# Gate projections of a merged three-branch block as seven half-sized products a gate

## The chip, the cores and the metric

The kernel runs on one core of one Trainium2 chip. A core has five engines with a queue of instructions each: TensorE (PE, matrix products), VectorE (DVE), ScalarE (ACT), GpSimd (POOL) and SyncE (SP, which issues most transfers). The metric is the device time of one execution in microseconds (us), as the median of several runs.

## What is computed

One layer of a decoder trunk on 512 tokens of 1024 features, in float32. Three token mixers give three branches of 512 features; each is mapped to 1024 features, weighted by a sigmoid gate computed from the normalised input, and the three are added. The change lies in the lines from `gates` to `merged`.

```python
h = rms_norm(x, g_mix)                       # 512 tokens x 1024
p = h @ w_in                                 # 1024 x 7680
q, fp, iv, go, bg, cg, xc, u, v, gates = jnp.split(p, offsets, axis=-1)
...
z = jnp.stack([o_a, o_b, o_c], axis=2)       # three branches of 512 features
y = jnp.einsum('bsnw,nwd->bsnd', z, w_branch)          # 3 x (512 -> 1024)
gate = jax.nn.sigmoid(gates).reshape(B, S, N_BRANCH, D)
merged = jnp.sum(gate * y, axis=2)
x = x + merged @ w_o
h2 = rms_norm(x, g_ffn)
x = x + jnp.square(jax.nn.relu(h2 @ w_ff1)) @ w_ff2
return rms_norm(x, g_final)
```

## The kernel before

Every float32 operand is split into a high part (rounded to the type fp32r, on ScalarE) and a low part (the rest, on VectorE), and a product of two operands takes three matmuls, high by high, high by low and low by high (`mm3`). A matmul has 128 partitions and 512 columns.

The work is a list of *units*. A unit is what one weight tile of 128 x 1024 is used for: 24 matmuls (8 pairs of blocks by 3). The main loop goes through the list. At unit i it lets ScalarE make the high part of the weights of unit i + 2, takes the result of unit i - 1 out of PSUM (its *take-in*), lets VectorE make the low part, issues the next loads on SP, and then issues the matmuls of unit i. Two tables of hooks add other work by hand: `pre` ahead of a unit's matmuls and `post` behind them. Each engine works through its queue in the order in which the loop writes it. Raw weight tiles (tag `raw`), high parts (`wh`) and low parts (`wl`) have three buffers each, PSUM accumulators (`acc`) eight; other tiles have one buffer with a name of its own (`x0`.., `z0`.., `h0`..), and who takes such a buffer again waits for its last reader.

In order, the units are: projections of the first mixers; 12 units of the short convolution; then, eight times (d is a block of 128 output features), three gate projections of one unit each, the products of branches 1 and 2 in one unit (`w_bc`) and that of branch 0 in half a unit (`w_a`); eight units of the output projection `w_o`; and the feed-forward stage. Gates and merged values are *feature-major*: features on the partitions, tokens along the columns. The merged block d is split into `mg`, and the output projection takes it as the stationary operand.

The normalised input is not stored. `xh` and `xl` hold x times `g_mix`, split; a gate's result is multiplied by `rb`, the reciprocal root mean square of each token along the columns, when it is taken in (`ev_gate`):

```python
tt(dve, g, a, rb, ALU.mult)
act.activation(g, g, AF.Sigmoid)
```

The feed-forward stage already uses seven products of half-sized blocks in place of eight, with weight sums formed by transfers that add to what is in a tile (issued by POOL, `accum_op`). Its output stage turns tiles from token-major to feature-major by transposes on PE, 16 in a group (`turn`), in two groups.

Of the kernel before, what the change touches and what calls it, by code (L numbers as in the profile page):

```python
# [11 lines left out]
ALU = mybir.AluOpType  # L12
# [21 lines left out]


@with_exitstack
def trunk_kernel(ctx: ExitStack, tc, xT, x_t, w_f, w_t, w_bc, w_a, w_o, w_1, w_2, vecs, rows, gfin, w_sg, cst, lmask, out):
# [522 lines left out]
    for d in range(KD):  # L560
        for n in (1, 2, 0):
            proj(28 + n * KD + d, lambda a, d=d, n=n: ev_gate(d, n, a))
        unit(w_bc[d], lambda w: (branch(w, 0, 1), branch(w, S, 2)), lambda a, d=d: ev_bc(d, a))
        unit(w_a[d], lambda w: branch(w, 0, 0), lambda a, d=d: ev_a(d, a), S)
# [603 lines left out]
```

## Time and profile before

| | before |
|---|---|
| device time, median of 3 runs | 829.73 us (828.86 to 830.4) |
| profiled execution: its device time, and its span | 829.05 us, 827.3 us |
| PE busy, matmuls | 816.8 us, 99% |
| PE busy, loading weights (PEld, beside the matmuls) | 682.6 us, 83% |
| VectorE busy | 543.8 us, 66% |
| ScalarE busy | 346.0 us, 42% |
| GpSimd busy | 156.2 us, 19% |
| bytes moved by transfers | 102.45 MB |

The profile is one execution, and its own device time lies 1.75 us above its span. A busy share is a mean over the span. Matmuls are pipelined, so that the printed length of one is longer than the distance from its start to the next one's.

### The profile page before, as it was taken

What the parts mean: (1) busy time and instruction counts of PE and PEld (TensorE: products, weight loads), DVE (VectorE), ACT (ScalarE), POOL (GpSimd) and SP (SyncE); (2) the same over time, 40 slices, a digit from 0 to 9 for tenths busy, and PEclk for the clock granted to TensorE, in tenths of its full rate; (3) what the DMA queues carried; (4) which work ended last, traced back from release to release, by engine and by line L of the source; (5) the groups of instructions that cost most, each with busy time, mean ns of one, the idle gap of its engine ahead of it and who ended that gap; (6) DMA issues with size and microseconds to landing.
All of it is one profiled execution on the core that took longest, in us unless ns stands there. A gap on an engine that the chain in (4) does not pass through costs nothing.

```text
span 827.3 us, 9867 instructions
## 1 busy us (share of the span) xinstructions
PE 816.8 (99%) x3798; PEld 682.6 (83%) x3798; DVE 543.8 (66%) x706; ACT 346.0 (42%) x519; POOL 156.2 (19%) x187
## 2 busy tenths in 40 slices
PE   9999999999999999999999999999999999999995
PEld 7888888888988888888888888888888888888884
DVE  7556999878664445544454445777777777777763
ACT  6567555354333223223232335343434343434332
POOL 4313555561220000000000010302020202020000
PEclk9999999999999999999999999999999999999998
DMA  8331232213113232232325345748393839383502
GB/s 312 124 103 52 76 107 72 77 52 102 58 58 103 94 110 90 90 96 95 115 89 204 103 156 149 216 116 238 93 247 88 248 87 246 89 239 96 162 1 101
DMA packets 30432, 102.45 MB, mean 124 GB/s; under 512 B 3505, under 2 KB 3889, under 8 KB 30385
## 3 DMA queue, kind: packets, MB, share of 16 engines
q1 hardware_dynamic: 20736, 67.45, 23.7%
q0 software_dynamic: 9360, 34.08, 16.8%
q8 instruction: 30, 0.49, 0.3%
q10 hardware_dynamic: 288, 0.29, 0.1%
q14 instruction: 18, 0.14, 0.1%
HBM read 99.71 MB, written 2.10 MB: 123 GB/s over the span
## 4 chain that ended last, share of the span: by engine, by line
PE 91%; DVE 4%; ACT 3%; issue 1%; POOLq 0%; POOL 0%; DVEq 0%; ACTq 0%
PE acc L98 28%; PE acc L100 28%; PE acc L99 28%; PE acc L1058 3%; PE acc L326 3%; DVE h L79 1%; DVE wl L79 1%; DVE h L307 1%; ACT h L257 1%; DVE h L270 0%; ACT wh L972 0%; PE acc L989 0%; ACT h L261 0%; PE acc L478 0%; PE acc L379 0%
## 5 line engine op out<-in xcount | busy, mean ns | idle before, releaser
L98 PE MATMUL acc<-x,wh 128*128 128x512 f32 x672 | 263.8, 393 | 0.3 <-DVE h L332 0.3
L100 PE MATMUL acc<-x,wl 128*128 128x512 f32 x672 | 261.6, 389 | 0.0
L99 PE MATMUL acc<-x,wh 128*128 128x512 f32 x672 | 261.5, 389 | 0.0
L972 ACT ACTIVATE wh<-raw 128x1024 fp32r<-128x1024 f32 (+1 forms) x114 | 116.7, 1026 | 239.6 <-PE acc L99 136.3
L79 DVE TENSOR_TENSOR wl<-raw,wh 128x1024 fp32r<-128x1024 f32 (+1 forms) x120 | 152.1, 1269 | 44.3 <-ACT wh L972 43.9
L100 PEld LDWEIGHTS acc<-x,wl 128*128 128x128 f32 x672 | 126.1, 188 | 26.5
L98 PEld LDWEIGHTS acc<-x,wh 128*128 128x128 f32 x672 | 126.2, 188 | 26.1 <-DVE h L332 0.5
L99 PEld LDWEIGHTS acc<-x,wh 128*128 128x128 f32 x672 | 126.2, 188 | 25.8 <-issue 0.2
L79 DVE TENSOR_TENSOR h<-h,acc 128x512 f32<-128x512 f32 x118 | 75.7, 682 | 11.1 <-PE acc L100 10.9
L79 DVE TENSOR_TENSOR z<-z,z 128x1024 fp32r<-128x1024 f32 x51 | 61.7, 1221 | 32.1 <-ACT z L766 32.1
L692 ACT ACTIVATE h<-tmp 128x512 f32<-128x512 f32 x32 | 20.3, 634 | 124.9 <-DVE tmp L691 124.9
L766 ACT ACTIVATE z<-z 128x1024 fp32r<-128x1024 f32 x51 | 53.1, 1052 | 45.7 <-PE acc L100 28.2
L79 DVE TENSOR_TENSOR h<-h,h 128x256 f32<-128x256 f32 (+4 forms) x89 | 66.8, 755 | 7.6 <-ACT h L745 3.6
L100 PE MATMUL acc<-z,h 128*128 128x512 f32 x184 | 71.6, 389 | 0.0
L99 PE MATMUL acc<-z,h 128*128 128x512 f32 x184 | 71.6, 389 | 0.0
L98 PE MATMUL acc<-z,h 128*128 128x512 f32 x184 | 71.6, 389 | 0.0
L79 DVE TENSOR_TENSOR tmp<-acc,rb 128x512 f32<-128x512 f32 x28 | 19.4, 691 | 79.0 <-PE acc L100 79.0
L762 POOL DMA_DIRECT2D z<-w x28 | 24.6, 877 | 232.5 <-DVE z L79 192.9
L79 POOL TENSOR_TENSOR tmp<-tmp,tmp 128x512 f32<-128x512 f32 x15 | 21.1, 1405 | 198.0 <-DVE tmp L79 185.9
L691 DVE SCALAR_TENSOR_TENSOR tmp<-acc,rb 128x512 f32<-128x512 f32 x32 | 22.0, 688 | 30.8 <-PE acc L100 30.8
L100 PEld LDWEIGHTS acc<-z,h 128*128 128x128 f32 x184 | 34.5, 188 | 7.3
L99 PEld LDWEIGHTS acc<-z,h 128*128 128x128 f32 x184 | 34.5, 188 | 7.2
(187 smaller groups left out, 1070.3 us busy)
## 6 DMA issues: line engine op xcount, KB each, us to landing
z<-w POOLq DMA_DIRECT2D x65, 512.0 KB, 6.5
raw<-w_f SPq DMA_DIRECT2D x52, 512.0 KB, 3.3
raw<-w SPq DMA_DIRECT2D x34, 512.0 KB, 5.3
raw<-w_bc SPq DMA_DIRECT2D x8, 512.0 KB, 3.3
raw<-w_o SPq DMA_DIRECT2D x8, 512.0 KB, 3.3
raw<-w_t SPq DMA_DIRECT2D x4, 512.0 KB, 3.2
raw<-w_a SPq DMA_DIRECT2D x8, 256.0 KB, 2.6
h<-x_t SPq DMA_DIRECT2D x4, 512.0 KB, 7.1
```

Of the source, the lines that this page charges most:

```text
L79: return e.tensor_tensor(out=o, in0=a, in1=b, op=op)
L98: pe.matmul(o, lh, rh, start=start, stop=False, skip_group_check=more)
L99: pe.matmul(o, lh, rl, start=False, stop=False, skip_group_check=more)
L100: pe.matmul(o, ll, rh, start=False, stop=stop, skip_group_check=more)
L257: act.activation(d["t1"], d["t1"], AF.Exp, scale=-1.0)
L326: pe.matmul(ps[:, cs(b)], kl[:, cs(b)], qk[:, cs(b)], start=True, stop=True)
L691: dve.scalar_tensor_tensor(out=t, in0=part["f", i], scalar=0.0, in1=part["r2b"], op0=ALU.max, op1=ALU.mult)
L692: act.activation(hf["a" if r < 2 else "b"][:, cs(r % 2, S)], t, AF.Square)
L762: pool.dma_start(wr[n, g], w_2[g, src[0], src[1]], accum_op=ALU.add)
L766: act.activation(hi, wr[src, g], AF.Copy)
L972: act.activation(hi[:, :n], raws[i][:, :n], AF.Copy)
L1058: pe.matmul(a4[t], lh, rh, start=j == 0 and rnd == 0, stop=j == KD - 1 and rnd == 2)
```

## The change

Each gate is now token-major (tokens on the partitions) and made by seven products. The normalised input X (512 x 1024) is cut into four blocks X11, X12, X21, X22 of 256 tokens x 512 features, and a gate's weights W into W11 to W22 of 512 features x 512 outputs. Four combinations of X blocks ("1" = X21 - X22, "2" = "1" - X11, "4" = "2" + X12, "3" = X11 - X21) and four sums of W blocks (t1 = W12 + W11, t2 = t1 + W22, t4 = t2 + W21, t3 = W12 + W22) are formed, and the products are, in the order of `G_ORDER`, p1 = X11 W11, p5 = "1" t1, p2 = X12 W21, p6 = "2" t2, p3 = "4" W22, p7 = "3" t3, p4 = X22 t4. Some are added to an accumulator that is left open in PSUM. Each has 24 matmuls.

For this x is loaded a second time, unsplit, 512 features at a time (*half* g = 0, 1; each holds half of every block's features) into the tiles h0 and h1 (`x_load`), normalised there (`x_norm`), and its seven combinations are formed and split into tiles h2 to h15 (`x_form`). SP loads the weight blocks (`g_load`) and a first block of a sum (`g_chain`, tags x0 to x7, which were the slots of `xh` and `xl` and are now in pairs), GpSimd adds blocks to it (`g_add`), and ScalarE and VectorE split each (`g_split`).

The order of the units behind the convolutions is now: four units of branch 1 (y1), the seven products of gate 1, those of gate 2, four units of branch 2 (y2), gate 0's seven, and five of branch 0 (y0, the last one halved). Branch products are token-major as well; `y_ev` and `merge_1` multiply and add. The merged tiles are transposed on PE (`m_turn`, two groups of 16) and split (`m_turned`) for the output projection. Loads of units are held back between y1 and gate 0 (`limit`). The host arranges the weights to match (`w_g`, `w_b`).

```diff
-    def ev_gate(d, n, a):
-        g = tmp()
-        part[n] = g
-        tt(dve, g, a, rb, ALU.mult)
-        act.activation(g, g, AF.Sigmoid)
...
-    def ev_bc(d, a):
-        for i, n in enumerate((1, 2)):
-            tt(dve, part[n], a[i], part[n], ALU.mult)
-        tt(pool, part[1], part[1], part[2], ALU.add)
-
-    def ev_a(d, a):
-        tt(dve, part[0], a, part[0], ALU.mult)
-        tt(dve, part[0], part[0], part[1], ALU.add)
-        mt = hslot(d, F32R)
-        act.activation(mt[:, :S], part[0], AF.Copy)
-        yield
-        tt(dve, mt[:, S:], part[0], f(mt[:, :S]), ALU.subtract)
-        mg.append((mt[:, :S], mt[:, S:]))
+    def x_load(g):
+        for i in range(2):
+            xr_[i] = hslot(i, F32)
+            for b in range(2):
+                nc.sync.dma_start(xr_[i][:, cs(b, S)], xT[4 * g + 2 * i + b])
+
+    def x_norm(g):
+        for b in range(4):
+            xv = xr_[b // 2][:, cs(b % 2, S)]
+            dve.scalar_tensor_tensor(out=xv, in0=xv, scalar=vcol(V_GMIX + 4 * g + b), in1=rb, op0=ALU.mult, op1=ALU.mult)
+
+    def x_form(g, *names):
+        def q(i, half):
+            return two(xr_[i])[:, :, half * 256:(half + 1) * 256]
+        for n in names:
+            if n in ("11", "12", "22"):
+                src = q(int(n[1]) - 1, int(n[0]) - 1)
+            else:
...
+                tt(dve, src, i0, i1, op)
+                xr_[n] = src
+            t = hslot(XT[g, n], F32R)
+            hi, lo = two(t[:, :S]), two(t[:, S:])
+            act.activation(hi, src, AF.Copy)
+            tt(dve, lo, src, f(hi), ALU.subtract)
+            xf[g, n] = (hi, lo)
...
+    def g_chain(n, kind, base):
+        for g in range(2):
+            gw[n, g, kind] = xpair(base + g, F32)
+            nc.sync.dma_start(gw[n, g, kind], w_g[n, g, 0, 1])
+
+    def g_add(n, kind, fi, c):
+        for g in range(2):
+            pool.dma_start(gw[n, g, kind], w_g[n, g, fi, c], accum_op=ALU.add)
...
+    def g_product(n, a, b, key, start):
+        if start:
+            part[key] = [acc() for _ in range(2)]
+        for j in range(2):
+            for g in range(2):
+                for p in range(2):
+                    ah, al = (x[:, p, cs(j)] for x in xf[g, a])
+                    bh, bl = (x[:, cs(p, S)] for x in gw[n, g, b, "r"])
+                    mm3(part[key][j], ah, al, bh, bl, start and g == 0 and p == 0, g == 1 and p == 1, not start)
+
+    G_ORDER = (("p1", "11", "11", "B", True), ("p5", "1", "t1", "C", True), ("p2", "12", "21", "A", True),
+               ("p6", "2", "t2", "B", False), ("p3", "4", "22", "C", False), ("p7", "3", "t3", "B", False),
+               ("p4", "22", "t4", "B", False))
...
+    def g_ev(p):
...
+            if p in ("p1", "p5"):
+                act.activation(v, a, AF.Copy)
+            elif p == "p6":
+                act.activation(v, a, AF.Copy, scale=-1.0)
+            elif p == "p4":
+                act.activation(v, a, AF.Sigmoid)
+            else:
+                tt(dve, v, v, a, ALU.subtract if p == "p7" else ALU.add)
+                act.activation(v, v, AF.Sigmoid)
...
+    def y_ev(n, c):
+        for t in range(4):
...
+            if n == 1:
+                act.activation(v, part["y"][t], AF.Copy)
+            else:
+                tt(dve, v, v, part["y"][t], ALU.mult)
+                tt(dve, m, m, v, ALU.add)
+
+    def merge_1():
+        for t in range(4):
+            tt(dve, mt[t], mt[t], gt[t], ALU.mult)
+
+    def m_turn(ks):
+        for k in ks:
+            part["m", k] = acc()
+            for t in range(4):
+                pe.transpose(part["m", k][:, cs(t)], mt[t][:, cs(k)], ident)
...
+    at(pre, y1 - 2, x_load, 0)
+    at(pre, y1 - 1, x_norm, 0)
+    at(pre, y1 - 1, x_form, 0, "11")
+    at(pre, y1, x_form, 0, "1", "2", "12")
+    at(pre, y1 + 1, x_form, 0, "4", "3", "22")
+    at(pre, y1 + 1, x_load, 1)
+    at(pre, y1 + 2, x_norm, 1)
+    at(pre, y1 + 2, x_form, 1, "11")
+    at(pre, y1 + 3, x_form, 1, "1")
+    at(pre, y1 + 4, x_form, 1, "2", "12")
+    at(pre, y1 + 5, x_form, 1, "4")
+    at(pre, y1 + 6, x_form, 1, "3", "22")
...
+    def g_sched(n, c, t3, first):
+        u = gu[n]
+        at(pre, u - 1, g_split, n, "11", W11)
+        at(pre, u, g_split, n, "t1", ("c",))
+        at(pre, u, g_add, n, "c", *W22)
+        at(pre, u + 1, g_split, n, "21", W21)
+        at(pre, u + 2, g_split, n, "t2", ("c",))
+        at(pre, u + 2, g_add, n, "c", *W21)
+        if first:
+            at(pre, u + 2, g_chain, n, "t3", t3)
+            at(pre, u + 2, g_add, n, "t3", *W22)
+        at(pre, u + 3, g_split, n, "22", W22)
+        at(pre, u + 4, g_split, n, "t3", ("t3",))
+        at(pre, u + 5, g_split, n, "t4", ("c",))
...
+    at(pre, u2, merge_1)
...
+    at(post, y0 + 3, m_turn, range(4))
+    at(pre, y0 + 4, m_turned, range(4))
+    at(post, o0, m_turn, range(4, KD))
+    at(pre, o0 + 1, m_turned, range(4, KD))
```

What that makes of the queues is shown at three places, as engine rows with the names that the program gives its tiles (a number behind a name only tells tiles of one name apart). First VectorE's queue behind the last convolution unit, before: `tmp<-acc,tmp` is the result of the convolution, `z` its low part, `wl` the low part of a unit's weights, and `tmp<-acc,rb` a gate that is taken in.

```order
L79 TENSOR_TENSOR tmp_2083<-acc_2099,tmp_2083 128x512
L79 TENSOR_TENSOR wl_2125<-raw_2040,wh_2124 128x1024
L79 TENSOR_TENSOR z_2128<-tmp_2083,z_2128 128x512
L79 TENSOR_TENSOR tmp_2162<-acc_2134,rb 128x512
L79 TENSOR_TENSOR wl_2160<-raw_2097,wh_2159 128x1024
L79 TENSOR_TENSOR tmp_2196<-acc_2168,rb 128x512
L79 TENSOR_TENSOR wl_2194<-raw_2132,wh_2193 128x512
```

The same place of the change, from the last low part of the heads (`z`) on. The tiles h_2032 and h_2035 are h0 and h1 with half 0 of x, normalised by the two rows of L540; h_2099 is "11", then come "1", "2" and "12".

```order
L85 TENSOR_TENSOR z_2092<-h_507,z_2092 128x512
L540 SCALAR_TENSOR_TENSOR h_2032<-h_2032,vec,rb 128x512 x2
L540 SCALAR_TENSOR_TENSOR h_2035<-h_2035,vec,rb 128x512 x2
L85 TENSOR_TENSOR h_2099<-h_2032,h_2099 128x512
L85 TENSOR_TENSOR tmp_2081<-acc_2104,tmp_2081 128x512
L85 TENSOR_TENSOR wl_2130<-raw_2038,wh_2129 128x1024
L85 TENSOR_TENSOR z_2133<-tmp_2081,z_2133 128x512
L85 TENSOR_TENSOR tmp_2137<-h_2032,h_2035 128x512
L85 TENSOR_TENSOR h_2139<-tmp_2137,h_2139 128x512
L85 TENSOR_TENSOR tmp_2142<-tmp_2137,h_2032 128x512
L85 TENSOR_TENSOR h_2144<-tmp_2142,h_2144 128x512
L85 TENSOR_TENSOR h_2147<-h_2035,h_2147 128x512
```

It goes on with a branch's weights, then "4", "3" and "22" of half 0, and half 1 of x (h_2199 and h_2202, again h0 and h1), its "11" and "1", and the split of W11, whose two tiles are raw_2207 and raw_2209.

```order
L85 TENSOR_TENSOR wl_2183<-raw_2102,wh_2182 128x1024
L85 TENSOR_TENSOR tmp_2186<-tmp_2142,h_2035 128x512
L85 TENSOR_TENSOR h_2188<-tmp_2186,h_2188 128x512
L85 TENSOR_TENSOR tmp_2191<-h_2032 128x512
L85 TENSOR_TENSOR h_2193<-tmp_2191,h_2193 128x512
L85 TENSOR_TENSOR h_2196<-h_2035,h_2196 128x512
L540 SCALAR_TENSOR_TENSOR h_2199<-h_2199,vec,rb 128x512 x2
L540 SCALAR_TENSOR_TENSOR h_2202<-h_2202,vec,rb 128x512 x2
L85 TENSOR_TENSOR h_2249<-h_2199,h_2249 128x512
L85 TENSOR_TENSOR tmp_2280<-h_2199,h_2202 128x512
L85 TENSOR_TENSOR h_2282<-tmp_2280,h_2282 128x512
L85 TENSOR_TENSOR wl_2286<-raw_2207,wh_2285 128x1024
```

Where VectorE had one take-in and one low part in each unit, the normalising, summing and splitting of x has moved in between, ahead of the low part of W11. Second, SP's queue at the same place, with what each transfer waits for in brackets (an engine, or a queue of transfers). Before, it holds a unit's weights each time:

```order
L964 DMA raw_2040<-w_f 128x1024 [waits DMAHW5_49,DVE_49]
L964 DMA raw_2097<-w_bc 128x1024 [waits DMAHW6_49,DVE_49]
L964 DMA raw_2132<-w_a 128x512 [waits DMAHW7_49,DVE_49,Activation_49]
L964 DMA raw_2166<-w_f 128x1024 [waits DMAHW0_49,DVE_49]
```

After, between the loads of branch 1 and those of W11 (raw_2207, raw_2209), it holds the first blocks of the chain (x_2150, x_2152) and half 1 of x:

```order
L1189 DMA raw_2102<-w_b 128x1024 [waits DMAHW6_49]
L572 DMA x_2150<-w_g 128x1024 [waits PE_49]
L572 DMA x_2152<-w_g 128x1024 [waits DMAHW7_49,PE_49]
L535 DMA h_2199<-xT 128x512 [waits DMAHW0_49,DVE_49,Activation_49]
L535 DMA h_2199<-xT 128x512 [waits DMAHW1_49]
L535 DMA h_2202<-xT 128x512 [waits DMAHW2_49,DVE_49]
L535 DMA h_2202<-xT 128x512 [waits DMAHW3_49]
L567 DMA raw_2207<-w_g 128x1024 [waits DMAHW4_49]
L567 DMA raw_2209<-w_g 128x1024 [waits DMAHW5_49]
```

The loads of half 1 wait for VectorE and ScalarE (the last readers of h0 and h1), and those of W11 stand behind them. Third, VectorE at the second product of gate 0 after the change: `z` are the gate tiles of branch 2, `x` the merged tiles, and the last two rows the low parts of gate 0's t1.

```order
L85 TENSOR_TENSOR z_2674<-z_2674,acc_2992 128x512
L85 TENSOR_TENSOR x_2237<-x_2237,z_2674 128x512
L85 TENSOR_TENSOR z_2675<-z_2675,acc_2993 128x512
L85 TENSOR_TENSOR x_2239<-x_2239,z_2675 128x512
L85 TENSOR_TENSOR z_2676<-z_2676,acc_2994 128x512
L85 TENSOR_TENSOR x_2241<-x_2241,z_2676 128x512
L85 TENSOR_TENSOR z_2677<-z_2677,acc_2995 128x512
L85 TENSOR_TENSOR x_2243<-x_2243,z_2677 128x512
L85 TENSOR_TENSOR wl_3065<-x_2848,wh_3064 128x1024
L85 TENSOR_TENSOR h_3069<-x_2850,h_3068 128x1024
```

At a gate unit before, VectorE had one take-in and one low part (the rows of L79 above); here eight operations of 512 columns stand ahead of the low part.

## Rows read from the trace of the kernel before

**Rows 1.** The page, part 1: busy time, share of the span, instructions.

```profile
PE 816.8 (99%) x3798; PEld 682.6 (83%) x3798; DVE 543.8 (66%) x706; ACT 346.0 (42%) x519; POOL 156.2 (19%) x187
```

**Rows 2.** Waits of TensorE: total us, times, longest us.

```profile
PE acc L989 <- DVE ones L982: 1.1, 1, 1.1
PE acc L98 <- DVE h L332: 0.3, 1, 0.3
```

**Rows 3.** Timeline of PE (start us, us, line): first projection and first transposes.

```profile
245.04 0.39 PE L98 MATMUL acc<-x,wh 128*128 128x512 f32 x1
...
468.08 0.38 PE L641 MATMUL acc<-cons,h 128*128 128x128 f32 x2
```

**Rows 4.** Two stretches: length, busy PE PEld DVE ACT POOL, PEclk, DMA, GB/s.

```profile
245.00:468.20 223.20, 223.20 (x987) 184.75 (x987) 105.94 (x118) 67.88 (x88) 10.32 (x8) 1.00 0.33 108
500.00:560.00 60.00, 60.00 (x266) 49.65 (x265) 45.65 (x56) 27.63 (x35) 8.19 (x12) 1.00 0.56 150
```

**Rows 5.** Timeline of PE around the second group of transposes.

```profile
491.61 1.91 PE L641 MATMUL acc<-cons,h 128*128 128x128 f32 x16
493.27 0.48 PE L98 MATMUL acc<-x,wh 128*128 128x512 f32 x1
493.59 0.40 PE L99 MATMUL acc<-x,wh 128*128 128x512 f32 x1
```

**Rows 6.** Timeline of VectorE: convolution units, take-ins, low parts, the last heads.

```profile
216.40 0.75 DVE L505 SCALAR_TENSOR_TENSOR tmp<-tmp,vec,tmp 128x512 f32<-128x512 f32 x1
217.07 1.22 DVE L79 TENSOR_TENSOR wl<-raw,wh 128x1024 fp32r<-128x1024 f32 x1
...
234.63 0.68 DVE L79 TENSOR_TENSOR h<-h,acc 128x512 f32<-128x512 f32 x1
236.00 0.69 DVE L79 TENSOR_TENSOR z<-h,z 128x512 fp32r<-128x512 f32 x1 [0.70 <-ACT z L85]
...
238.91 0.69 DVE L79 TENSOR_TENSOR tmp<-acc,tmp 128x512 f32<-128x512 f32 x1 [0.23 <-PE acc L100]
...
247.02 0.68 DVE L79 TENSOR_TENSOR tmp<-acc,tmp 128x512 f32<-128x512 f32 x1
247.62 1.22 DVE L79 TENSOR_TENSOR wl<-raw,wh 128x1024 fp32r<-128x1024 f32 x1
248.75 0.68 DVE L79 TENSOR_TENSOR z<-tmp,z 128x512 fp32r<-128x512 f32 x1
```

**Rows 7.** Timelines of ScalarE and PE at the same units.

```profile
213.85 1.06 ACT L972 ACTIVATE wh<-raw 128x1024 fp32r<-128x1024 f32 x1 [4.66 <-PE acc L99]
214.86 0.72 ACT L503 ACTIVATE tmp<-tmp,vec 128x512 f32<-128x512 f32 x1
235.34 0.63 ACT L85 ACTIVATE z<-h 128x512 fp32r<-128x512 f32 x1 [1.89 <-DVE h L79]
238.71 0.49 PE L402 MATMUL acc<-cons,h 128*128 128x128 f32 x3
```

**Rows 8.** Transfers by target: count, KB each, median us from issue to landing.

```profile
raw<-w_f SPq DMA_DIRECT2D x52, 512.0 KB, 3.3
raw<-w_a SPq DMA_DIRECT2D x8, 256.0 KB, 2.6
...
z<-xT SPq DMA_DIRECT2D x7, 256.0 KB, 5.2
```

**Rows 9.** Line 762, adding transfers of the feed-forward stage: issue in ns, landing in us.

```profile
L762 POOL DMA_DIRECT2D z<-w x28: 857/877/907, 497.7 to 770.7; - x28
...
DMA to landing us min/median/max: 5.2/5.7/8.6
```

**Rows 10.** PE's last matmul, and the windows behind it (columns as in rows 4).

```profile
817.77 0.39 PE L100 MATMUL acc<-z,h 128*128 128x512 f32 x1
822.20:822.60 0.40, 0.00 (x0) 0.00 (x0) 0.00 (x0) 0.00 (x0) 0.00 (x0) 0.79 0.00 0
822.60:827.00 4.40, 0.00 (x0) 0.00 (x0) 0.00 (x0) 0.00 (x0) 0.00 (x0) 0.50 0.31 119
```

More of the change, by code (lines that the diff above doesn't have):

```diff
@@ L36, in trunk_kernel @@
 @with_exitstack
-def trunk_kernel(ctx: ExitStack, tc, xT, x_t, w_f, w_t, w_bc, w_a, w_o, w_1, w_2, vecs, rows, gfin, w_sg, cst, lmask, out):
+def trunk_kernel(ctx: ExitStack, tc, xT, x_t, w_f, w_t, w_g, w_b, w_o, w_1, w_2, vecs, rows, gfin, w_sg, cst, lmask, out):
     nc = tc.nc
@@ L536, in ev_a, with two @@
-    def ev_a(d, a):
-        tt(dve, part[0], a, part[0], ALU.mult)
-        tt(dve, part[0], part[0], part[1], ALU.add)
-        mt = hslot(d, F32R)
-        act.activation(mt[:, :S], part[0], AF.Copy)
-        yield
-        tt(dve, mt[:, S:], part[0], f(mt[:, :S]), ALU.subtract)
-        mg.append((mt[:, :S], mt[:, S:]))
+    xr_ = {}
+    xf = {}
+    XT = dict(zip([(g, n) for g in range(2) for n in ("11", "12", "1", "2", "4", "3", "22")], range(2, 16)))
+    def two(ap):
+        return ap.rearrange("p (b c) -> p b c", b=2)
@@ new lines, in x_load @@
+    def x_load(g):
[14 more added lines that the diff above has]
+            else:
+                t = tmp()
+                src = two(t)
+                i0, i1, op = {"1": (q(0, 1), q(1, 1), ALU.subtract), "2": (xr_.get("1"), q(0, 0), ALU.subtract),
+                              "4": (xr_.get("2"), q(1, 0), ALU.add), "3": (q(0, 0), q(0, 1), ALU.subtract)}[n]
+                tt(dve, src, i0, i1, op)
[5 more added lines that the diff above has]
+            xf[g, n] = (hi, lo)
@@ new lines, in g_product @@
+    def g_product(n, a, b, key, start):
+        if start:
+            part[key] = [acc() for _ in range(2)]
+        for j in range(2):
+            for g in range(2):
+                for p in range(2):
[5 more added lines that the diff above has]
+               ("p4", "22", "t4", "B", False))
@@ new lines, in trunk_kernel @@
+    gt = [None] * 4
+    mt = [None] * 4
+    def g_ev(p):
+        if p == "p1":
+            for t in range(4):
+                gt[t] = zpair(4 + t, F32)
+        key, row, col = {"p1": ("B", 0, 0), "p5": ("C", 1, 1), "p2": ("A", 0, 0), "p6": ("B", 0, 1), "p3": ("C", 0, 1),
+                         "p7": ("B", 1, 1), "p4": ("B", 1, 0)}[p]
+        for j in range(2):
+            v = gt[2 * row + j][:, cs(col, S)]
+            a = part[key][j]
+            if p in ("p1", "p5"):
[7 more added lines that the diff above has]
+                act.activation(v, v, AF.Sigmoid)
@@ new lines, in y_mm, with mm @@
+    def y_mm(n, j, ks):
+        def mm(w):
+            if j == 0:
+                part["y"] = [acc() for _ in range(4)]
+            for k2 in ks:
+                k = 2 * j + k2
+                for t in range(4):
+                    mm3(part["y"][t], zt[n][k][0][:, cs(t)], zt[n][k][1][:, cs(t)], w[0][:, cs(k2, S)], w[1][:, cs(k2, S)],
+                        k == 0, k == 3)
+        return mm
+    def y_ev(n, c):
+        for t in range(4):
+            if n == 1 and c == 0:
+                mt[t] = xpair(t, F32)
+            v, m = (mt[t] if n == 1 else gt[t])[:, cs(c, S)], mt[t][:, cs(c, S)]
+            if n == 1:
+                act.activation(v, part["y"][t], AF.Copy)
+            else:
+                tt(dve, v, v, part["y"][t], ALU.mult)
+                tt(dve, m, m, v, ALU.add)
@@ new lines, in merge_1, with m_turned @@
+    def merge_1():
+        for t in range(4):
+            tt(dve, mt[t], mt[t], gt[t], ALU.mult)
+    def m_turn(ks):
+        for k in ks:
+            part["m", k] = acc()
+            for t in range(4):
+                pe.transpose(part["m", k][:, cs(t)], mt[t][:, cs(k)], ident)
+    def m_turned(ks):
+        for k in ks:
+            h = hslot(k, F32R)
+            act.activation(h[:, :S], part["m", k], AF.Copy)
+            tt(dve, h[:, S:], part["m", k], f(h[:, :S]), ALU.subtract)
+            mg.append((h[:, :S], h[:, S:]))
@@ L559, in trunk_kernel, with g_units @@
         proj(12 + c, lambda a, c=c: ev_bg(c, a))
[L560 to L564, printed above, removed]
+    y1 = len(units)
+    for c in range(2):
+        for j in range(2):
+            unit(w_b[1, c, j], y_mm(1, j, range(2)), (lambda a, c=c: y_ev(1, c)) if j else None)
+    phase1 = len(loads)
+    gu = {}
+    def g_units(n):
+        gu[n] = len(units)
+        for o in G_ORDER:
+            units.append((None, lambda w, o=o: g_product(n, *o[1:]), lambda a, o=o: g_ev(o[0])))
+    g_units(1)
+    g_units(2)
+    y2 = len(units)
+    for c in range(2):
+        for j in range(2):
+            units.append((("y2", c, j), y_mm(2, j, range(2)), (lambda a, c=c: y_ev(2, c)) if j else None))
+    g_units(0)
+    y0 = len(units)
+    for c in range(2):
+        for j in range(2):
+            if c and j:
+                load(len(units) - 2, w_b[0, c, j])
+                units.append((len(loads) - 1, y_mm(0, j, range(1)), None))
+                units.append((len(loads) - 1, y_mm(0, j, range(1, 2)), lambda a, c=c: y_ev(0, c)))
+            else:
+                unit(w_b[0, c, j], y_mm(0, j, range(2)), (lambda a, c=c: y_ev(0, c)) if j else None)
     at(pre, 3, sg_rows)
@@ new lines, in trunk_kernel, with L @@
+    at(pre, y1 + 1, x_form, 0, "4", "3", "22")
[6 more added lines that the diff above has]
+    at(pre, y1 + 6, x_form, 1, "3", "22")
+    W11, W12, W21, W22 = (0, 0), (0, 1), (1, 0), (1, 1)
+    def L(slot, n, *what):
+        for g, w in what:
+            at(pre, slot, g_load, n, g, *w)
+    def g_sched(n, c, t3, first):
[12 more added lines that the diff above has]
+        at(pre, u + 5, g_split, n, "t4", ("c",))
+        at(pre, u - 1, g_load, n, 1, *W21)
+        at(pre, u - 1, g_load, n, 0, *W22)
+        at(pre, u + 1, g_load, n, 1, *W22)
@@ new lines, in g_early @@
+    def g_early(n, s_c, s_t3, c, t3):
+        at(pre, s_c, g_chain, n, "c", c)
+        at(pre, s_c + 1, g_add, n, "c", *W11)
+        if s_t3 is not None:
+            at(pre, s_t3, g_chain, n, "t3", t3)
+            at(pre, s_t3, g_add, n, "t3", *W22)
+    u1, u2, u0 = gu[1], gu[2], gu[0]
+    g_early(1, y1, None, 4, 6)
+    L(y1 + 1, 1, (0, W11), (1, W11), (0, W21))
+    g_sched(1, 4, 6, True)
+    L(u1 + 1, 2, (0, W11))
+    L(u1 + 3, 2, (1, W11), (0, W21))
+    g_early(2, u1 + 4, u1 + 6, 6, 4)
@@ L610, in trunk_kernel @@
+    g_sched(2, 6, 4, False)
+    at(pre, u2, merge_1)
+    at(pre, u2 + 1, y2_load, 0, 0)
+    at(pre, u2 + 3, y2_load, 0, 1)
+    at(pre, u2 + 3, y2_load, 1, 0)
+    at(pre, y2 - 2, y2_split, 0, 0)
+    at(pre, y2 - 2, y2_load, 1, 1)
+    at(pre, y2 - 1, y2_split, 0, 1)
+    L(y2 - 1, 0, (0, W11))
+    at(pre, y2, y2_split, 1, 0)
+    L(y2, 0, (1, W11))
+    at(pre, y2 + 1, y2_split, 1, 1)
+    L(y2 + 1, 0, (0, W21))
+    g_early(0, u2 + 5, u2 + 7, 4, 6)
+    g_sched(0, 4, 6, False)
     x2, x2h, x2l = [], [], []
@@ L958, in trunk_kernel @@
     issued = [0]
+    limit = [phase1]
     def issue():
-        if issued[0] < len(order):
+        if issued[0] < limit[0]:
             src, n = loads[order[issued[0]]]
@@ L966, in issue, with issue_more @@
             issued[0] += 1
+    def issue_more(n):
+        limit[0] = len(order)
+        for _ in range(n):
+            issue()
+    at(pre, u0 + 1, issue_more, 1)
+    at(pre, u0 + 3, issue_more, 2)
     def split_hi(i):
```

52 lines of the change are left out of this document (36 added, 16 removed).

## The prediction

> **What bounds the kernel now.** I read the page first, then TensorE's waits, then the stretch that the change rewrites. On the page the reader is to see TensorE (PE) busy for 99% of the span and VectorE (DVE) far below it [rows 1]; in the view of waits, that PE waited for VectorE once for 1.1 us at the start and hardly again [rows 2]. In the stretch from the last convolution projection (PE goes on at 245.04) to the first transposes of the output stage (468.08) PE issues 984 matmuls of 512 columns without a gap: 24 gate projections of 24, branch products of 288 in all, five output units of 24. So one matmul costs 223.04 / 984 = 0.2267 us [rows 3], at the full granted clock, with VectorE under half busy [rows 4]. Here the time is the number of matmuls times 0.2267 us; whatever else runs there is free until PE waits for it.
>
> **What the change removes and adds on PE.** A gate now takes seven products of 24 matmuls where it took eight projections of 24: 3 x 24 = 72 fewer, 72 x 0.2267 = **16.3 us** gained. The branch products stay at 288, transposed in role. New are 32 transposes of the merged tiles, in two groups of 16. Before has two such groups; the second starts at 491.61 and the next matmuls at 493.27 and 493.59, where a running stream would have 0.23 between them: 1.66 + 0.09 = 1.75 us a group, **3.5 us** lost [rows 5]. If PE never waited, 829.05 - 16.3 + 3.5 = 816.2 us.
>
> **What has to be on time for that.** Prices on VectorE, start to start: 0.60 us for 512 columns, 1.13 for 1024, 0.67 for a scalar-tensor-tensor of 512; on ScalarE (ACT) 1.01 for 1024. A value that goes VectorE, ScalarE, VectorE takes 1.37 from first start to last start. VectorE starts 0.2 us after PE turns to the next unit [rows 6, 7]. 54 weight tiles of 1024 columns (42 for the products, 12 for the branches) are now split into a high part on ScalarE and a low part on VectorE; before it was 32 and 8 halves. Both engines get more work in less time, and the question is only where it ends last.
>
> *Steady products.* While one product runs (24 x 0.2267 = 5.44 us), the two engines take in the one before (two tiles) and split two weights of the next. With the take-in on VectorE that is 0.2 + 0.60 + 0.68 + 0.63 (the second sigmoid) + 1.01 + 1.13 = some 4.7 us for the first weight, and PE can use it before the second, which it needs 6 matmuls (1.36 us) later. 4.7 is below 5.44: hidden. Only products 2, 3 and 7 take in on VectorE, so a chain late by some tenths recovers. In the feed-forward stage VectorE is busy 45.65 of 60 us and PE still runs all 60 [rows 4]. I price steady products at 0; if the cover goes, each pays the excess over 5.44.
>
> *The start of gate 1: the stall.* VectorE must normalise x again (8 operations), form 7 combinations for each half of the features (14 low parts, 8 sums) and split W11, before PE may begin the first product, while PE has only four branch units (4 x 5.44 us from 245.04: it is through at 266.8). I walk VectorE's queue in the order shown above, from the rows of before up to 247.0, where its work for the heads ends [rows 6]:
> - four normalisations to 249.7, the low part of "11" to 250.3, the last convolution result and a branch split to 252.0, its low part to 252.6. PE needs this one at about 253.6: no stall.
> - half 0's "1" and "2" (sum, ScalarE, low part: 1.97 each) and "12" to 257.2; a branch split to 258.7; "4" and "3", 1.97 each, and "22" to 263.3.
> - half 1 of x goes into the same two tiles h0 and h1, so SP's loads wait for their last readers: h0 is free at 261.3, h1 at 263.3. A load of 256 KB landed in 2.6 us [rows 8], so the tiles are there at about 264 and 266; SP's loads of W11 stand behind them in its queue and land by 269.
> - normalisations to 267.3, "11" to 267.9, "1" with ScalarE between to 269.9.
> - the high part of W11 on ScalarE 269.2 to 270.2, the low part on VectorE to 271.4. The first product's second matmul reads it.
>
> PE would have issued that matmul at 267.0: **4.4 us** lost. What is unknown is the landing: with 5.2 us, as x took when the queues were full at the start [rows 8], it would be 7.0. I take 2.6, because the stretch moves 108 GB/s on average [rows 4]. From below, if the loads cost nothing, VectorE's own work still ends about 270: 3 us.
>
> Behind it every product of gate 1 has its split in time by the same walk: the second one's low part is there just as PE asks for it, the third's and later ones a microsecond ahead.
>
> *Merging.* Product 1 of gate 2 shares VectorE with the four 1024-wide multiplications of the first merge (4.5 us); these stand behind its split, and the next one ends about 0.6 us ahead of PE: 0. After branch 2's last unit eight operations of 512 (mult and add, 1.30 a pair, 5.2 us) stand ahead of the split for gate 0's second product: 0.2 + 5.2 + 1.2 = 6.6 us, and PE asks at 5.44 + 0.23. **1.0 us** lost.
>
> *Transposes.* The first group needs the merge of the left columns, done 5.4 us into a stretch in which PE still has 36 matmuls (8.2 us): 0. The second needs the last eight merge operations, 5.4 us from the end of branch 0, against the first output unit's 5.44 us: 0.1. The copies back (four of 0.6 on either engine) are used one unit later: 0.
>
> *Accumulating transfers.* The sums of weight blocks are made by transfers that GpSimd (POOL) issues: 0.88 us for one, 5.7 in the median to landing, 8.6 at most [rows 9]. The walk leaves 8.8 us from issue to need for gate 1's second split of the chain, 7.4 for its t3 (which stands behind two other adds on POOL), 10.9 and 8.9 for the chains of gates 2 and 0. At the median: 0. At 8.6 throughout: 1.2 us, for t3.
>
> **Sum.** 829.05 - 16.3 + 3.5 + 4.4 + 1.0 + 0.1 = 821.7 us against the profiled execution (its span of 827.3 and 1.75 around it). The median of the runs shown is 829.73, 0.7 higher, so I forecast **822.4**.
>
> **Rivals.**
> *The clock falls in the stall.* The last matmul ends at 817.77 + 0.39 = 818.16. The granted clock is 0.79 in the mean of 822.2 to 822.6 and 0.5 (1.2 GHz) from there, so it left the full level (2.4 GHz) at about 822.4, after 4.3 us without work [rows 10]. The stall that I expect is a gap of 3.2 us, one matmul, and 1.2 us: near that. If the clock falls, matmuls take 0.453 us until it rises; no row shows how long that is. Bounds: nothing, and as long as the fall took (4.3 us at half pace, 2.15 lost): 822.4 + 2.2 = 824.6. For it: a late landing makes the gap longer. Against: the lone matmul. The Trainium skill, TensorE: Matmul & The Clock Gate, section Why this matters for your kernels, asks that a kernel leave no such gaps between bursts, since the clock drops; the trace agrees at the kernel's end only, and by that rule this rival's 824.6 would be the time.
>
> *No stall.* VectorE and the loads keep up at the start: then 829.73 - 16.3 + 3.5 = 816.9. For it: before, PE never waited here. Against: VectorE's queue alone, from rows with hardly any spread.
>
> *Late sums, slower than before.* Each microsecond beyond 7.4 (t3 of gate 1) and beyond 8.8 and 8.9 (the chains of gates 1 and 0) stops PE for a microsecond. Faster turns into slower when they cost 7.3 us more, and into slower by over 0.2% at 9.0: from 10.9 us on the chain of gate 2 is late too, so 4 L - 36.0 = 9.0, L = 11.3 us, twice the median. At 12 us it is 822.4 + 12.0 = 834.4. For it: here they come in pairs, two tiles at once, and run beside SP's weight loads, and where the transfers run behind, all splits after them do. Against: the largest in the trace is 8.6, in a stage that moves 150 GB/s.
>
> **How the numbers follow.** My forecast (820 to 824) 0.46; the clock falls or the loads of x land late (824 to 827.5) 0.18; no stall or a small one (816.5 to 820) 0.12; late sums 0.14, of it 0.02 with a gain left, 0.04 within 0.2% of before and 0.08 slower; waits that I did not see 0.10, of it 0.04, 0.03 and 0.03. Faster is 0.46 + 0.18 + 0.12 + 0.02 + 0.04 = 0.82, same 0.07, slower 0.11. 0.2% of 829.7 is 1.7 us, about what a measurement of this kernel can tell from no change. Range 817.5 to 827.5: it leaves out the late sums and the bare no-stall case.
>
> **What would show it.** Right: in the list of waits PE waits 3 to 5 us for the splits (VectorE's and ScalarE's) at about 267, and about 1 us at the second product of gate 0, and nowhere else; products at 0.2267 us a matmul; VectorE's queue at 267 just past the second normalisation. Wrong: PE waiting in each product (the steady chain is longer than 5.44), ScalarE's splits held by GpSimd's transfers, a granted clock of 0.5 behind the stall, or no wait at 267.

## The result and the profile after

The changed kernel takes 835.37 us in the median of 4 runs (833.78 to 837.66), the kernel before 829.3 (828.6 to 830.4): ratio 1.0073, 95% interval 1.0057 to 1.0088. It is slower by 0.7%, where 822.4 was forecast. The profiled execution is the slowest of the four, 837.66 us, 8.61 above the profiled one of before.

The head of the page after, against [rows 1]:

```profile
PE 813.0 (97%) x3758; PEld 676.9 (81%) x3758; DVE 574.9 (69%) x748; ACT 381.7 (46%) x573; POOL 165.4 (20%) x203
PEclk9999999999999889999999999999999999999999
q0 software_dynamic: 12816, 46.67, 25.2%
q1 hardware_dynamic: 22176, 72.69, 24.3%
```

PE has fewer matmuls and is busy for less of a longer span, and its clock is down in slices 14 to 16. The last two rows (packets, MB, share of 16 engines) are GpSimd's queue of transfers and SP's. PE's waits after (total, times, longest), against [rows 2]:

```profile
PE acc L104 <- ACT wh L590: 7.1, 2, 4.4
PE acc L104 <- DVE z L85: 3.6, 2, 1.8
PE acc L105 <- DVE wl L85: 1.5, 2, 0.8
```

L590 is a weight's high part, L85 a low part or a take-in. Where these waits stand is seen on PE's timeline (start us, us, line, what it waited for in brackets). The steady distance from start to start is still 0.2267 us; what lies above it is lost.

```profile
266.88 0.39 PE L106 MATMUL acc<-wh,z 128*128 128x512 f32 x1
271.67 0.50 PE L104 MATMUL acc<-wh,h 128*128 128x512 f32 x1 [4.40 <-ACT wh L590]
272.93 0.79 PE L105 MATMUL acc<-wl,h 128*128 128x512 f32 x1 [0.76 <-DVE wl L85]
...
302.63 0.39 PE L106 MATMUL acc<-wh,h 128*128 128x512 f32 x1
305.71 0.50 PE L104 MATMUL acc<-wh,h 128*128 128x512 f32 x1 [2.69 <-ACT wh L590]
306.97 0.80 PE L105 MATMUL acc<-wl,h 128*128 128x512 f32 x1 [0.76 <-DVE wl L85]
...
355.25 0.39 PE L106 MATMUL acc<-wh,h 128*128 128x512 f32 x1
357.43 0.47 PE L104 MATMUL acc<-wh,h 128*128 128x512 f32 x1 [1.79 <-DVE z L85]
357.74 0.39 PE L105 MATMUL acc<-wl,h 128*128 128x512 f32 x1
```

- **Start of gate 1**, 266.88 to 279.02: (4.79 - 0.23) + (1.26 - 0.23) = 5.6 us of waiting, and 2.9 at the lower clock: 8.5.
- **p7 of gate 1**, which needs t3, 302.63 to 316.46: 2.85 + 1.03 + 1.03 of waiting, and 4.2 at the lower clock: 9.1.
- **p4 of gates 2 and 0**, at 355.25 and 417.22: 2.04 us each.

829.05 - 16.3 + 3.5 + 8.5 + 9.1 + 4.1 = 838.0 us, against 837.66. The gain and the transposes are as forecast (443.97 to 445.63, and 0.32 to the next matmul: 1.75 a group); four stalls took the gain and more.

The clock in windows (length, busy us of PE, PEld, DVE, ACT, POOL, granted clock, share of the DMA engines, GB/s):

```profile
267.30:271.60 4.30, 0.00 (x0) 0.00 (x0) 3.31 (x5) 1.56 (x3) 0.00 (x0) 1.00 0.76 301
272.90:278.60 5.70, 5.67 (x13) 4.46 (x14) 4.83 (x6) 5.22 (x9) 0.31 (x1) 0.50 0.53 184
280.00:290.00 10.00, 10.00 (x46) 8.27 (x45) 5.59 (x7) 6.76 (x10) 0.28 (x1) 1.00 0.92 220
307.00:315.00 8.00, 7.53 (x16) 5.14 (x17) 3.90 (x5) 4.18 (x5) 1.34 (x2) 0.50 0.57 152
358.00:368.00 10.00, 10.00 (x46) 8.25 (x45) 2.45 (x2) 3.64 (x5) 1.73 (x2) 1.00 0.99 274
```

The clock is still 1.00 while PE waits and 0.50 (1.2 GHz) behind the lone matmul; there matmuls stand 0.43 us apart. The waits at p4, 1.8 us without work each, leave it at 1.00 (last row).

### The profile page after: what moved, and what is told of

Its sections match the earlier page's. It is cut to its first block, busy times and chain, and to the rows that moved or that the text cites. A ratio compares the mean times of both kernels' runs of the same rounds, so it can differ in the third digit from the quotient of the medians.

```text
span 835.9 us, 9960 instructions
## 1 busy us (share of the span) xinstructions
PE 813.0 (97%) x3758; PEld 676.9 (81%) x3758; DVE 574.9 (69%) x748; ACT 381.7 (46%) x573; POOL 165.4 (20%) x203
## 4 chain that ended last, share of the span: by engine, by line
PE 81%; issue 6%; DVE 4%; DMA 4%; ACT 3%; POOL 0%; SPq 0%; POOLq 0%; DVEq 0%; ACTq 0%
PE acc L104 25%; PE acc L105 24%; PE acc L106 24%; DMA x<-w_g 3%; PE acc L332 3%; PE acc L1291 3%; DVE h L85 1%; DVE wl L85 1%; DVE h L313 1%; ACT h L263 1%; DVE h L276 0%; ACT wh L1205 0%; ACT h L267 0%; PE acc L484 0%; PE acc L385 0%
## 5 line engine op out<-in xcount | busy, mean ns | idle before, releaser
L104 PE MATMUL acc<-x,wh 128*128 128x512 f32 x480 | 189.2, 394 | 0.3 <-DVE h L338 0.3
L106 PE MATMUL acc<-x,wl 128*128 128x512 f32 x480 | 187.0, 390 | 0.0
L105 PE MATMUL acc<-x,wh 128*128 128x512 f32 x480 | 186.9, 389 | 0.0
L85 DVE TENSOR_TENSOR wl<-raw,wh 128x1024 fp32r<-128x1024 f32 (+1 forms) x107 | 133.3, 1252 | 68.0 <-ACT wh L1205 47.3
L1205 ACT ACTIVATE wh<-raw 128x1024 fp32r<-128x1024 f32 x82 | 86.0, 1052 | 136.7 <-PE acc L105 51.6
L106 PEld LDWEIGHTS acc<-x,wl 128*128 128x128 f32 x480 | 90.1, 188 | 18.9
L104 PEld LDWEIGHTS acc<-x,wh 128*128 128x128 f32 x480 | 90.2, 188 | 18.6 <-DVE h L338 0.5
L105 PEld LDWEIGHTS acc<-x,wh 128*128 128x128 f32 x480 | 90.2, 188 | 18.3 <-issue 0.2
L104 PE MATMUL acc<-wh,h 128*128 128x512 f32 x208 | 83.2, 400 | 10.7 <-ACT wh L590 7.1
L105 PE MATMUL acc<-wl,h 128*128 128x512 f32 x208 | 83.5, 401 | 1.5 <-DVE wl L85 1.5
L85 DVE TENSOR_TENSOR z<-z,z 128x1024 fp32r<-128x1024 f32 x51 | 61.6, 1220 | 32.1 <-ACT z L988 32.1
L85 DVE TENSOR_TENSOR h<-h,acc 128x512 f32<-128x512 f32 x118 | 75.7, 682 | 11.0 <-PE acc L106 10.9
L106 PE MATMUL acc<-wh,h 128*128 128x512 f32 x208 | 83.0, 399 | 0.0
L85 DVE TENSOR_TENSOR h<-h,h 128x256 f32<-128x256 f32 (+4 forms) x95 | 70.9, 750 | 7.6 <-ACT h L967 3.6
L104 PEld LDWEIGHTS acc<-wh,h 128*128 128x128 f32 x208 | 40.2, 193 | 20.6 <-ACT wh L590 7.9
L105 PEld LDWEIGHTS acc<-wl,h 128*128 128x128 f32 x208 | 40.3, 194 | 10.5 <-DVE wl L85 2.1
```

Source lines behind the costliest of these rows:

```text
L1205: act.activation(hi[:, :n], raws[i][:, :n], AF.Copy)
```

## The experiments

Two theories stood against each other. **A:** each stall has a cause of its own and can be taken away by itself. **B:** the transfers bound the whole stretch (the DMA engines' share is 0.92 from 280 to 290 us, above), and what is won at one product is lost at the next. Against B stands the last row above: at a share of 0.99, PE worked all 10 us.

**Own tiles for half 1 of x.** `e1`:

```diff
-            xr_[i] = hslot(i, F32)
+            xr_[i] = xpair(6 + i, F32) if g else hslot(i, F32)
-            elif i == 3:
-                hi, lo = xpair(6, F32R), xpair(7, F32R)
```

> Edit: half 1 of x is loaded into tiles x6 and x7, which are free, and no longer into h0 and h1; the second tile of gate 1's t1 takes h0 and h1 for its split in exchange. The order of VectorE's queue is unchanged. Theory A (the four stalls have causes of their own): VectorE's waits for these loads (0.68 + 0.25 + 1.32 = 2.25 us) go, so the stall at the first product shrinks from 8.5 us to about 5 (3.3 of waiting, 1.7 at the lower clock); and the chain for t3, which waited until the end of p5 for x6 and x7, starts sooner, which takes 4 to 9 us off the second stall. In all 823 to 828 us. Theory B (the transfers bound the whole stretch, 250 GB/s wanted): what is gained at the start is lost again at later products, 834 to 836 us. If VectorE's own queue sets the start (rival to the loads), the first stall stays above 7.

835.53 us, ratio 1.0062 (1.0041 to 1.0082). In its profile the first stall is 4.7 us, as expected, and that of t3 8.2: SP still issues t3's first blocks at 284.4, behind weight loads that wait for buffers. The time does not move. 1.8 us of this profile were lost ahead of the rewritten stretch, 1.2 of them in the first 30 us, where PE waited twice for the kernel's first weights, as in other profiles of the study; what took the gain in its other runs stays open.

**Matmuls in the gap.** `e2`, behind the last branch-1 unit:

```diff
+    def fill():
+        a = acc()
+        for i in range(18):
+            pe.matmul(a, zt[1][0][0][:, :P], zt[1][1][0], start=True, stop=True)
+    at(post, y1 + 3, fill)
```

> Edit: 18 matmuls of 512 columns into an unused accumulator are put between the last branch-1 unit and gate 1's first product (18 x 0.227 = 4.1 us of the gap of 4.56). They compute nothing that is used. If the gap without work is what took TensorE's clock down, the granted clock stays at 1.00 from 270 to 280 us and the 14 slow matmuls (0.427 in place of 0.227) give back 2.8 us: 832.6 us. If the clock falls for another reason (the lone matmul and the second gap of 1 us, or the load of the transfers), 835.4 us.

834.23 us, 1.0063 (1.0040 to 1.0086). PE's timeline:

```profile
272.00 0.50 PE L104 MATMUL acc<-wh,h 128*128 128x512 f32 x1
273.26 0.50 PE L105 MATMUL acc<-wl,h 128*128 128x512 f32 x1 [0.76 <-DVE wl L85]
273.60 0.39 PE L106 MATMUL acc<-wh,h 128*128 128x512 f32 x1
```

The windows over the filler and behind it (columns as above):

```profile
267.82:272.00 4.18, 4.18 (x19) 3.19 (x17) 3.23 (x6) 1.62 (x3) 0.00 (x0) 1.00 0.89 345
273.60:278.60 5.00, 5.00 (x24) 4.14 (x23) 4.12 (x6) 4.90 (x8) 0.00 (x0) 1.00 0.62 210
```

The lone matmul and the second wait are there as before, the transfers are as dense (0.89), and the clock stays at 1.00: without the 4.4 us without work it does not fall here. The 2.9 us come back in the trace (filler and waits together lose 5.3, where waits and lower clock lost 8.5); the time moves by less than the intervals can tell.

**Take-in of p7 earlier.** `e3`:

```diff
-        at(pre, u + 5, g_split, n, "t4", ("c",))
+        at(pre, u + 5, g_split, n, "t4", ("c",), (0,))
+        at(post, u + 5, g_ev, "p7", (0,))
+        at(post, u + 5, g_split, n, "t4", ("c",), (1,))
+        at(post, u + 5, g_ev, "p7", (1,))
...
-    at(pre, y2 - 2, y2_split, 0, 0)
+    at(post, y2 - 2, y2_split, 0, 0)
...
```

> Edit: the take-in of p7 is put between the splits of t4's two tiles: first accumulator, split of the second tile, second accumulator, and behind that the split of branch 2's first weights. If p4 waits because it adds to the accumulators that p7's take-in still has to read, and that take-in stands behind splits in VectorE's queue, both waits of 2.04 us go: 835.4 - 4.1 = 831.3 us. If p4 then waits for the second t4 tile instead, 833 to 835 us. Theory B (transfers bound the stretch): 835 us.

832.3 us in 10 runs (830.0 to 836.94), 1.0041 (1.0023 to 1.0059): 3.1 us less, and the two intervals just touch. The p4 of gates 2 and 0 lose 0.37 us each in place of 2.04. What stood ahead of the take-in is seen on VectorE's timeline in the changed kernel. `z<-z,acc` is the take-in, whose first accumulator was complete 12 matmuls before 355.48, at 352.8, and `wl<-raw` a branch-2 weight for later:

```profile
352.57 1.23 DVE L85 TENSOR_TENSOR wl<-x,wh 128x1024 fp32r<-128x1024 f32 x1 [1.65 <-ACT wh L590]
353.71 1.22 DVE L85 TENSOR_TENSOR h<-x,h 128x1024 fp32r<-128x1024 f32 x1
355.46 1.23 DVE L85 TENSOR_TENSOR wl<-raw,wh 128x1024 fp32r<-128x1024 f32 x1 [0.53 <-ACT wh L91]
356.60 0.68 DVE L85 TENSOR_TENSOR z<-z,acc 128x512 f32<-128x512 f32 x1
```

**Without the adds of gate 1's t3.** `e4` leaves out `at(pre, u + 2, g_add, n, "t3", *W22)` in `g_sched`.

> Edit: the two adds that make gate 1's t3 are left out (its t3 is W12 alone, so this gate is not the reference's). Theory A: the second stall (9.07 us) is these two transfers alone, so 835.4 - 9.1 = 826.3 us, or 828 if p4's wait for the take-in then shows in gate 1 too. Theory B: the transfers are behind as a whole, and c's third sum or the next gate's loads come late in its place, 830 us or more.

829.11 us in 10 runs, 0.9994 (0.9983 to 1.0005): 6.3 less. The stall at p7 is gone, and no other transfer is late in its place: A, not B, for this stall.

**Plain transfers in place of adding ones.** `e5`:

```diff
-            pool.dma_start(gw[n, g, kind], w_g[n, g, fi, c], accum_op=ALU.add)
+            pool.dma_start(gw[n, g, kind], w_g[n, g, fi, c])
```

> Edit: GpSimd's transfers of weight blocks write in place of adding (same places, same bytes, same waits; the sums are wrong, so the gates are not the reference's). If adding is what makes these transfers slow, their landing falls from 7.1 us in the median (14.7 at most) towards the 5.3 of SP's plain loads into the same tiles, the second stall (9.07) shrinks below 3 us and the time to about 829 us. If it is only that many transfers run at once, landings stay at 7 and 12 or more and the time at 835 us.

827.91 us, 0.9972 (0.9962 to 0.9982): 7.5 less, with the stall at p7 gone. The line that issues them in the changed kernel (issue in ns, minimum, median, maximum; then landing in us):

```profile
L576 POOL DMA_DIRECT2D x<-w_g x24: 854/863/1179, 247.3 to 402.7; - x24
DMA to landing us min/median/max: 5.2/7.1/14.7
```

And in this one:

```profile
L576 POOL DMA_DIRECT2D x<-w_g x24: 527/527/754, 248.0 to 391.2; - x24
DMA to landing us min/median/max: 3.6/4.7/7.5
```

The same bytes at the same places land 2.4 us sooner in the median and 7.2 at worst. It is the adding that makes these transfers slow, and what runs beside them too (SP's `raw<-w_g` land in 4.5 us in the median, 5.8 with the adding).

**VectorE's queue reordered.** `e7`, with half 1 in tiles of its own:

```diff
+    at(pre, y1, x_load, 1)
+    at(pre, y1, x_sums, 0)
...
+    at(pre, y1 + 2, x_sums, 1)
+    at(pre, y1 + 2, x_form, 1, "1")
+    at(pre, y1 + 4, x_form, 1, "2", "12", "4", "3", "22")
```

> Edit: half 1 of x in tiles of its own as in the run before, loaded as soon as the convolutions are through; the four sums of a half are made back to back, so that ScalarE's high parts run beside them and VectorE doesn't wait for each; of half 1 only 11 and 1 stand ahead of the split of W11, the rest behind it. Theory A: VectorE then reaches W11's low part before 266.8 us, the start stall (8.5 us, 4.7 with the tiles alone) goes to under 1, and the lower clock with it; t3's stall of some 8 us stays: 835.4 - 8.5 = 827 us. Theory B (transfers bound the stretch): PE comes sooner to sums that are not there yet, and most of the gain is lost at t3: 832 us or more.

830.03 us, 1.0008 (0.9993 to 1.0023): 5.3 less. The start loses 0.89 us in place of 8.5; t3 still costs 6.6 and the p4 of gates 2 and 0 2.04 each. The time lies between the two theories' numbers; the trace has A's stalls and no new one.

**All three.** `e8` adds the take-in and issues t3's first blocks one product sooner (`at(pre, u + 1, g_chain, n, "t3", t3)`).

> Edit: the reordering, the take-in of p7 ahead of the second t4 split, and gate 1's t3 chain loaded one product sooner. Theory A: all three losses go, 835.4 - 8.5 - 4.1 - (7 to 9) = 814 to 816 us, near the 816.9 of the forecast's case without waits. Theory B: the sums still land 10 to 12 us behind their issue and PE waits for one of them in gate 1, 820 to 826 us.

830.54 us in 10 runs (825.51 to 832.56), 1.0008 (0.9992 to 1.0023): no gain over `e7`. A fell here as to t3: even in the fastest run, the profiled one of 825.51, p7 loses 6.4 us and p6 (t2) 1.4. Where the other runs lost up to 7 us more, no trace shows. An earlier place in the queue does not help where the sums themselves land in 7.1 us in the median and up to 11.0.

**t3 summed on GpSimd.** `e9`, in place of six adding transfers:

```diff
+    def t3_sum(n):
+        for g in range(2):
+            tt(pool, gw[n, g, "t3"], gw[n, g, "t3"], gw[n, g, 1, 1], ALU.add)
```

> Edit: as the kernel with all three, and t3 of every gate is added by GpSimd itself from the W22 tiles that are there for p3, in place of adding transfers (6 transfers of 512 KB fewer; two adds of 1024 columns on GpSimd, some 2.8 us each by its 1.41 us for 512). Theory A: nothing waited any more, so as the kernel with all three within 1 us; Theory B: with a twelfth less to move, 2 to 5 us faster than it. If GpSimd's adds disturb VectorE or come late, slower by 1 to 5 us.

824.27 us, 0.9945 (0.9928 to 0.9963): 6.3 less than `e8`. 4.4 us are lost at 290.73 now, at p3, where no sum is wanted: 2.8 of waiting, and 1.6 at the lower clock behind it. GpSimd's timeline there:

```profile
287.54 5.05 POOL L85 TENSOR_TENSOR x<-x,raw 128x1024 f32<-128x1024 f32 x2
```

VectorE's, with a quiet pair of low parts first, and then the two of p3's weights one by one:

```profile
274.88 2.36 DVE L85 TENSOR_TENSOR wl<-raw,wh 128x1024 fp32r<-128x1024 f32 x2 [0.52 <-ACT wh L592]
...
289.53 4.15 DVE L85 TENSOR_TENSOR wl<-raw,wh 128x1024 fp32r<-128x1024 f32 x1 [1.65 <-ACT wh L592]
...
293.61 1.21 DVE L85 TENSOR_TENSOR wl<-raw,wh 128x1024 fp32r<-128x1024 f32 x1
```

Two low parts take 5.29 us here, and 2.36 without the adds. All of the difference lies in the first: it starts while GpSimd adds and ends at 293.68, 1.09 us behind the end of GpSimd's two adds, while the second takes 1.21 as usual. At gates 2 and 0 the low part that starts beside the adds takes 3.24 and 3.80 us and ends 1.1 behind them too.

**t3 on VectorE; then t1 too.** `e10` has `tt(dve, ...)` for the same sums, and three of half 1's sums behind W11's split; `e11` makes t1 of gates 2 and 0 so as well.

> Edit: as the kernel with the reordering, the take-in and the early t3, but t3 of every gate is added by VectorE from the W22 tiles (two operations of 1024, 2.3 us a gate), and three of half 1's four sums stand behind the split of W11. Theory: the adding transfers of t3 were too slow, and GpSimd's adds slowed VectorE (5.29 us in place of 2.36 for two low parts of 1024 beside them); with neither, the stall of 4.4 us at 291 goes, and the start (0.9 us) too: 824.3 - 5.3 = 819 us. Rival: VectorE itself becomes late with 2.3 us more a gate, 822 to 825 us.

822.06 us, 0.9911 (0.9896 to 0.9926), 3 us above the theory's 819, at the lower edge of the rival's range. The stalls at p3 and at the start are gone, as expected; the losses left are 1.72 (p5 of gate 1), 1.02, 1.49 and three of 0.3 to 0.4.

> Edit: as the run before, and t1 of gates 2 and 0 is added by VectorE from the W11 tiles too, in place of four adding transfers (another 2.3 us of VectorE a gate). If what is left is late transfers, the same or up to 1 us faster than the run before; if VectorE is by now the engine that is late, 1 to 4 us slower.

822.42 us, 0.9905 (0.9889 to 0.9921): no difference from the run before.

**Other orders.** `e12`, on `e10`: gate 1's t1 split ahead of the forms of half 1, half of the first merge a product earlier, and the sigmoid behind the high part of t4's second tile.

```diff
-    at(pre, u2, merge_1)
+    at(pre, u1 + 6, merge_1, (0, 1))
+    at(pre, u2, merge_1, (2, 3))
```

> Edit: the run with t3 on VectorE, in other orders: gate 1's t1 split stands ahead of the rest of half 1's combinations; half of the first merge stands one product earlier; the sigmoid of p7's first accumulator stands behind the high part of the second t4 tile. By the trace of that run the waits left in the stretch are 1.72 (p5), 1.02 (gate 1's p4), 1.49 (gate 2's p2) and 0.3 to 0.4 three times; these orders should take the three large ones: 822.1 - 4.2 = 818 us. If transfers are what is late there, 820 to 822 us.

817.27 us, 0.9853 (0.9836 to 0.9869). The page's busy times:

```profile
PE 805.0 (99%) x3758; PEld 671.4 (82%) x3758; DVE 580.6 (71%) x754; ACT 381.6 (47%) x573; POOL 160.7 (20%) x197
```

PE's only wait in the rewritten stretch:

```profile
PE acc L105 <- DVE wl L85: 0.4, 1, 0.4
```

The stalls are gone, and the time is the 816.9 us that the forecast's case without waits gave, within 0.4; against the 829.19 of the kernel before beside it, 11.9 us are gained of the 12.8 of that case. The three orders were not tried one by one, and the kernel differs from the change by more than order: t3 is no longer summed by transfers.

## Why the prediction was wrong, point by point

- **Where the 16 us come from.** The profiled execution took 837.66, and the sum gave 821.7 for it: 4.1 us more at the start, 9.1 at t3 and 4.1 at p4, and 1.1 of small terms that were not paid, 16.2 us in all against 16.0.
- **PE's sum** (16.3 us less, 3.5 for the transposes) held: the stretch adds up with it, and the last run comes within 0.9 us of it.
- **Accumulating transfers** is the step that failed most. It priced them at the median of [rows 9], 5.7 us, and took the 8.6 there for an upper end. GpSimd issued four adds in a row here, and the last of them, for t3's second tile, took 14.7 us (GpSimd's timeline, then the chain of waits):

```profile
290.88 0.85 POOL L576 DMA_DIRECT2D x<-w_g  x1 [10.59 <-DVE wl L85]
292.01 2.64 POOL L576 DMA_DIRECT2D x<-w_g  x3 [0.28 <-DVE h L85]
```

```profile
293.57 14.72 DMA x<-w_g
```

  The rival *Late sums* had the place (t3 first) and the mechanism, with a chance of 0.14; t3 came 14.7 - 7.4 = 7.3 us late by its own count. PE waited 4.9 us for it, and the clock of the next point nearly doubled what it lost. With adds the kernel takes 835.4, without 827.9. A warning was to be had before: a gate moves 18 tiles of 512 KB in 7 x 5.44 us, 248 GB/s, where the forecast leaned on a stage of 150 [rows 4]. The bytes alone are not the cause: with plain transfers they are the same, and the stall is gone.
- **Steady products at 0** failed at p4. p4 adds to the accumulators that p7's take-in still reads, so PE needs that take-in first. The walk had take-ins only as work ahead of a split. It cost 4.1 us, and moving the take-in gave 3.1 back.
- **The start** was right in place and cause, and too small: 5.6 us of waiting in place of 4.4. The mis-sized term is the landing of half 1, taken at 2.6 us: the loads of x landed in 3.1 in the median and 3.9 at most, and VectorE could go on with h1 only at 267.38, where the walk had it there at about 266:

```profile
267.38 1.42 DVE L540 SCALAR_TENSOR_TENSOR h<-h,vec,rb 128x512 f32<-128x512 f32 x2 [1.32 <-DMA h<-xT]
```

  So half 1's "1" was late, and W11's high part, which stands behind it on ScalarE, began at 270.57 (269.2 in the walk); the low part came at 272.8 (271.4 forecast).
- **The clock** was kept as a rival, at 2.2 us and a chance of 0.18 together with late loads. It came true at the start, for 2.9 us, and again at t3 for 4.2. The filler shows that the time without work causes it. By the rule of the Trainium skill that the prediction weighed (TensorE: Matmul & The Clock Gate, section Why this matters for your kernels) it had to fall there; the trace agrees, with 0.50 behind 4.4 us without work. Less did it too: at t3 2.7 us without work, one matmul and 0.8 more; in `e1` 1.8 us, one matmul and 0.8 more (matmuls stand 0.43 us apart behind both); in `e9` one wait of 2.6 us. The 1.8 us ahead of p4, with steady work behind them, did not.
- **1.0 us at gate 0's second product** was wrong. VectorE began the eight operations at 382.91, 1.84 us before PE left the unit (384.75): its four accumulators are complete one after another. The walk had started them 0.2 behind its end. The low part starts at 388.22, and PE is not held. VectorE's timeline:

```profile
382.91 0.69 DVE L85 TENSOR_TENSOR z<-z,acc 128x512 f32<-128x512 f32 x1 [1.08 <-PE acc L106]
...
387.61 0.69 DVE L85 TENSOR_TENSOR x<-x,z 128x512 f32<-128x512 f32 x1
388.22 1.22 DVE L85 TENSOR_TENSOR wl<-x,wh 128x1024 fp32r<-128x1024 f32 x1
```

Open: why single runs of the changed kernel differ by 3.9 us. The stall at t3 differs between profiles (7.3 us in the filler's, 9.1 in the change's), but no run isolates it.

## What to carry to other kernels

A product that saves TensorE an eighth of its matmuls pays only while the engines beside it can serve what is left: add up the bytes that the new stage moves in its own time, and price each kind of transfer by itself, adding ones above all, which were late here where plain ones with the same bytes were not. Where a product adds to an open accumulator, its predecessor's take-in is on the critical path and belongs ahead of any split for later. A long wait can be paid twice: 4.9 us of waiting at t3 cost another 4.2, because the matmuls behind it ran at half the clock.

## What the hardware showed unexpectedly

- A transfer that adds costs more than the same bytes written: GpSimd issues it in 0.86 us in place of 0.53, it lands in 7.1 us in place of 4.7 in the median, and up to 14.7 in place of 7.5.
- GpSimd's adds of two tensors in SBUF hold up VectorE's operations on two such tensors: a low part of 1024 columns that starts beside them takes 3.2 to 4.2 us in place of 1.2 and ends 1.1 us behind them, in all three gates. GpSimd's pair of adds takes 5.1 us each time. The Trainium skill, GPSIMD Engine Reference, section Specifications, says that the two share their interfaces to SBUF and contend when VectorE reads two inputs from there; the trace agrees.
